# RWKV-7, S5 and ConvFFN layer: inverses in 32x32 blocks, gathered state stores, PSUM banks taken later, and a planner that may hold VectorE

## Chip, cores and metric

The kernel runs on one core of a Trainium2 chip, in one launch. Times are device microseconds of that core; lower is better. Three runs were timed, and one more execution was profiled.

## What is computed

One decoder layer for a prompt of 1024 tokens and 8 sample tokens, all in f32:

```python
proj = rmsnorm(x) @ w_in                 # columns: RWKV | S5 input u | two gates
# RWKV-7, 8 heads x 64, one step per token:
sa = einsum('bhvk,bhk->bhv', S, -kk)
S  = S * w[:, :, None, :] + sa[..., None] * (kk * a)[:, :, None, :] + v[..., None] * k[:, :, None, :]
y  = einsum('bhvk,bhk->bhv', S, r)
# S5, 32 groups x 64 complex states:  s_t = A s_{t-1} + B u_t,  y = Re(C s) + D u
z  = gelu(ys) @ w_glu
x += (sigmoid(g_rw) * rw_out + sigmoid(g_s5) * s5_out) @ w_out
x += (gelu(causal_conv3(a_up)) * b_up) @ w_ffn_out
x += sigmoid(rmsnorm(x) @ w_ple_gate) * (p @ w_ple)
```

It returns the final RMSNorm and the new states, among them the last S5 state of the prompt (`ssm_p`, real and imaginary part) and of the samples (`ssm_s`).

## The kernel before

**Layout.** Features lie on partitions, tokens on the free axis (1032 of them). Every large product is split into high and low halves of its operands, three matmuls for one (`psm<-h1h,whi`, `psm<-h1l,whi`, `psm<-h1h,wlo`): weights are loaded as `wraw`, rounded to `whi` on ScalarE, and the rest `wlo` is made on GpSimd.

**Order of the work.** The code doesn't issue instructions. It records them in a planner, class `Sched` (lines 103 to 420), with a cost, a priority and what they depend on. `run` (line 350) takes the engine that can issue first and, of its instructions that are ready at that moment, the one with the smallest priority number; `issue` (line 374) books its cost. So each engine gets one fixed order, and on the chip it follows it strictly. Every recorded instruction is emitted at line 411, so all have this line in the profile, and tiles tell them apart. All DMAs are issued by SP, also in one order. A DMA is charged a fixed part before and after its bytes. A tile of a pool gets its buffer when the first instruction that names it is issued; `pb` is a pool of three PSUM banks (tag `big`).

**Stages.** First the input projection runs as 34 column tiles (`psm<-h1...`), and beside it the S5 part (`build_s5`, line 970): set-up of the discretisation on VectorE (`s_...`), a scan in levels (`cmac`, lines 1172 to 1182), then for each of four quarters a product (`yp`), a store and read-back through DRAM that changes the layout (`yq<-ys`, `yf<-yq`), a GELU (`zt`), and a store (`zd`). The pool `sp` of S5 must be free before the RWKV part can start (line 720).

**RWKV** (`build_rwkv`, line 1270) goes over 8 units, 4 head pairs x 2 halves of 512 tokens, of 8 chunks of 64 tokens. `stage_a` (line 1328) makes the scaled operands `AR` and `BK`. `stage_g` (line 1399) multiplies them to `Gm`, a 128x128 matrix for each chunk and head, and transposes `BK` and `v` (`tpp`, `vpp`). The upper left 64x64 block of each of the 16 matrices of a unit is then inverted (unit triangular): it is stored to DRAM (`ld`), read back as rows that stand on all partitions that need them (`Lj`), 63 steps on VectorE update `Tm`, a step of several columns as a product into `Tt` and a sum, and the result goes through DRAM again (`xd`) back into `Gm`. `chain` (line 1459) walks the chunks one after another, TensorE and VectorE by turns (`chp`, `pe`, `UV`, `S`); its second product `chp<-pe,Gm` needs the inverse. `post` (line 1509) normalises and gates the unit's result; its gate product is `gps`. The preparation of unit n+1 may run beside the chain of unit n, and both stand ahead of the wide matmuls of the large products, which fill TensorE in between.

**The rest.** S5's GLU (`psm<-zh`), then the output projections and the FFN in two parts of tokens (`parts`, line 751), the first beside the last RWKV units. The RWKV pools must be free before the second part.

Of the kernel before, what the change touches and what calls it, by code (L numbers as in the profile page):

```python
# [58 lines left out]
def _const_cols():  # L59
    c = 0  # L60
    for name, n in (("ident", 128), ("mask", 128), ("bo", 128), ("i64", 64),
                    ("scan", HW), ("tinit", 512), ("ones", 128)):
        CONSTS[name] = (c, n)
        c += n
    return c
# [5 lines left out]
def _consts():  # L71
    out = np.zeros((P, NCON), np.float32)

    def put(name, a):
        c, n = CONSTS[name]
        out[:, c:c + n] = a

    put("ident", np.eye(P))
    i, t = np.arange(64)[:, None], np.arange(64)[None, :]
    put("mask", np.tile(np.concatenate([i < t, i <= t], 1), (2, 1)))  # L80
    put("ones", np.full((P, P), 1.0 / D))
    b = np.kron(np.eye(2), np.ones((64, 64)))
    put("bo", b)
    put("i64", np.tile(np.eye(64), (2, 1)))
    s = np.ones((P, HW))
    s[:, ::CH] = 0
    put("scan", s)

    ti = np.zeros((P, 8, 64))
    for p in range(P):  # L90
        for c in range(8):
            ti[p, c, 8 * c + p // 16] = 1
    put("tinit", ti.reshape(P, 512))
    return out
# [7 lines left out]
class Sched:  # L102
# [10 lines left out]
    SWITCH = 90  # L113
    SETS = {"Exp": (0, 6), "Tanh": (0, 11), "Ln": (5, 6), "Gelu_apprx_tanh": (11,), "Sin": (9,)}
# [235 lines left out]
    def run(self, until):  # L350
        pend, free = self.pend, self.free
        while not until():
# [17 lines left out]
            r, o = min(((c[0], c[1]) for c in cand if c[0] <= t + 1e-6),  # L370
                       key=lambda c: (c[1].prio, c[1].seq))
            self.issue(t, o)

    def issue(self, t, o):
# [17 lines left out]
        if e == "SP":  # L392
            st = max(self.dma_free, t + 700)
            self.dma_free = st + o.tail
            end = self.dma_free + 1000
        else:
            end = t + o.lat
# [572 lines left out]
def build_s5(g, sp, pb, cp, I, O, Ud, Zd, pcs, dscr, dap, dma):  # L970
# [236 lines left out]
    dma(O["ssm_s"][0], er)  # L1207
    dma(O["ssm_s"][1], ei)
# [57 lines left out]
    dma(O["ssm_p"][0], Xr[:, :, 127])  # L1266
    dma(O["ssm_p"][1], Xi[:, :, 127])


def build_rwkv(g, rp, pb, pch, py, I, O, Pd, Wd, Ad, Yd, sg, ssh, omu, pc, pcs, dscr, dap, dma,  # L1270
# [23 lines left out]
    def big(name):  # L1294
        return pb.tile([P, HW], F32, name=name, tag="big")
# [103 lines left out]
    def stage_g(p, hf, a):  # L1399
# [4 lines left out]
        fl = lambda z: z.rearrange("p a b -> p (a b)")  # L1404
        for c4 in range(0, NC, 4):
            gp = [big(f"gp{h}").rearrange("p (c t) -> p c t", t=P) for h in range(2)]
            for j in range(4):
                for h in range(2):
                    hs = slice(64 * h, 64 * h + 64)
                    T.matmul(gp[h][:, j], fl(BK[hs, c4 + j]), fl(AR[hs, c4 + j]),  # L1410
                             start=True, stop=True)
# [3 lines left out]
            for j in range(4):  # L1415
                T.transpose(tp[:, j], fl(BK[:, c4 + j]), ident)
            S.activation(BT[:, c4:c4 + 4], tp, AF.Copy)
            vp = big("vpp").rearrange("p (c t) -> p c t", t=P)
            for c in range(c4, c4 + 4):
                if c == 0:  # L1420
                    T.matmul(vp[64:128, 0], v[:, 0:CH], ident, start=True, stop=True)
                else:
                    T.transpose(vp[:, c - c4], v[:, (c - 1) * CH:(c + 1) * CH], ident)
            S.activation(UV[64:128, c4:c4 + 4], vp[64:128], AF.Copy)

        ld = dscr_ring("ld")
        dma(dap(ld, 0, [[64, 64], [4096, 2 * NC], [1, 64]]),
            Gm[0:64, :, :, 0:64].rearrange("p a b t -> p (a b) t"))
        Tm = rp.tile([P, 8, 64], F32, name="Tm", tag="Tm", bufs=2)
        tmp = rp.tile([P, 8, 64], F32, name="Tt", tag="Tt", bufs=2)  # L1430
        dma(Tm, I["con"][:, nc_:nc_ + 512].rearrange("p (a b) -> p a b", b=64))
        JB = 4
        for j0 in range(0, 63, JB):
            L = rp.tile([P, JB, 64], F32, name="Lj", tag="Lj", bufs=4)
            dma(L, dap(ld, j0 * 64, [[0, 8], [4096, 16], [1, JB * 64]]))
            for j in range(j0, min(j0 + JB, 63)):
                n, w = j // 8 + 1, 63 - j
                if n < 3:
                    for c in range(n):
                        V.scalar_tensor_tensor(Tm[:, c, j + 1:], L[:, j - j0, j + 1:],  # L1440
                                               Tm[:, c, j:j + 1], Tm[:, c, j + 1:],
                                               op0=MUL, op1=ADD)
                    continue
                V.tensor_tensor(tmp[:, :n, :w], L[:, None, j - j0, j + 1:].to_broadcast([P, n, w]),
                                Tm[:, :n, j:j + 1].to_broadcast([P, n, w]), op=MUL)
                V.tensor_tensor(Tm[:, :n, j + 1:], Tm[:, :n, j + 1:], tmp[:, :n, :w], op=ADD)
        xd = dscr_ring("xd")
        dma(dap(xd, 0, [[64, P], [8192, 8], [1, 64]]), Tm)
        dma(Gm[0:64, :, :, 0:64].rearrange("p a b t -> p (a b) t"),
            dap(xd, 0, [[1024, 64], [64, 2 * NC], [1, 64]]))  # L1450
# [4 lines left out]
    def dscr_ring(name):  # L1455
        ring[name] = ring.get(name, -1) + 1
        return dscr(f"{name}{ring[name]}", [16, 64, 64])
# [51 lines left out]
    def post(p, c0, w, parts, bv):  # L1509
# [15 lines left out]
        G.tensor_tensor(y, y, q, op=MUL)  # L1525
# [3 lines left out]
        T.matmul(gp[:, :w], g2[:, p * P:(p + 1) * P], sg[:, c0:c0 + w], start=True, stop=True)  # L1529
# [3 lines left out]
    def sample(p, a):  # L1533
# [6 lines left out]
        t1 = rp.tile(sh, F32, name="st1", tag="Tt", bufs=2)  # L1540
# [169 lines left out]
```

## Time and profile before

| what | before |
|---|---|
| median of 3 runs | 1969.66 us |
| lowest and highest | 1963.52, 1975.32 us |
| the profiled execution | 1970.79 us |
| its span, first to last instruction | 1969.0 us |
| mean granted TensorE clock | 0.963 |
| data moved | 236.69 MB, 181247 packets |

The profiled execution lies 1.13 us above the median. Busy times of engines overlap, so they don't add up to the span. A granted clock of 1.00 is 2.4 GHz, 0.50 is 1.2 GHz; a number in between is the mean over a stretch. In the rows below PE is TensorE, PEld its weight load, DVE is VectorE, ACT ScalarE, POOL GpSimd, and SPq the queue of SP that issues the DMAs. An f32 matmul stands in the trace as two instructions.

### The profile page before, as it was taken

The page shows a single profiled execution, that of the slowest core. Times are in us where ns is not written, and L with a number is a line of the kernel's source. Part 1 is how long each engine was busy: PE and PEld are TensorE (multiplying, and loading weights), DVE is VectorE, ACT ScalarE, POOL GpSimd, SP SyncE. Part 2 cuts the span into 40 slices and gives each one's busy share as a digit, 9 for nine tenths or more (in the row PEclk, how much of TensorE's full clock was granted, in tenths as well). Part 3 has the DMA queues.
Part 4 walks back from the last instruction along what each step waited for, and adds up shares of the span by engine and source line. Part 5 has one row for each costly group of instructions (what it writes and reads, how often), then busy time and mean ns, then how long its engine had stood idle before and what let it go on. Part 6 is the DMA issues. An engine that isn't in the chain of part 4 may idle for free.

```text
span 1969.0 us, 31981 instructions
## 1 busy us (share of the span) xinstructions
PE 1841.3 (94%) x11392; PEld 1621.4 (82%) x11392; DVE 1305.3 (66%) x2803; ACT 839.6 (43%) x1453; POOL 833.0 (42%) x1127
## 2 busy tenths in 40 slices
PE   6999769989989999999998999999989999999987
PEld 5988758968888798777676777787889999999987
DVE  8999225867777698986898965546464444435465
ACT  5222334215523542456562455435445333233364
POOL 4453124203322241373653445656554444444454
PEclk9998879969999999999999999999999999999988
DMA  5554973433342554532423223633342333333222
GB/s 183 154 173 134 132 237 122 128 91 99 114 142 81 182 170 147 184 121 72 130 90 115 80 79 104 221 97 96 92 151 76 97 92 92 95 89 98 88 77 84
DMA packets 181247, 236.69 MB, mean 120 GB/s; under 512 B 56400, under 2 KB 104784, under 8 KB 180944
## 3 DMA queue, kind: packets, MB, share of 16 engines
q1 hardware_dynamic: 181088, 234.65, 39.7%
q8 instruction: 90, 1.47, 0.3%
q14 instruction: 69, 0.57, 0.1%
HBM read 189.75 MB, written 45.02 MB: 119 GB/s over the span
## 4 chain that ended last, share of the span: by engine, by line
PE 63%; DVE 13%; DMA 13%; ACT 4%; issue 4%; POOL 2%; SPq 2%; DVEq 0%; ACTq 0%; POOLq 0%
PE psm L411 53%; PE chp L411 4%; DVE Tm L411 3%; DMA yf<-yq 2%; DVE Tt L411 2%; PE Yps L411 2%; PE gp L411 2%; SPq L411 2%; POOL wlo L411 1%; DMA Lj<-ld 1%; DMA Gm<-xd 1%; DMA wraw<-in_w_ffn_in 1%; DMA xd<-Tm 1%; DVE x L411 1%; ACT L411 1%
## 5 line engine op out<-in xcount | busy, mean ns | idle before, releaser
L411 POOL TENSOR_TENSOR wlo<-wraw,whi 128x512 fp32r<-128x512 f32 (+2 forms) x468 | 594.9, 1274 | 684.4 <-ACT whi L411 645.4
L411 PE MATMUL psm<-act,whi 128*128 128x260 f32 (+1 forms) x2880 | 666.5, 324 | 4.9 <-ACT whi L411 1.5
L411 PEld LDWEIGHTS psm<-act,whi 128*128 128x128 f32 x2880 | 478.9, 190 | 50.4 <-ACT whi L411 4.4
L411 ACT ACTIVATE whi<-wraw 128x512 fp32r<-128x512 f32 (+2 forms) x468 | 279.3, 599 | 560.8 <-PE psm L411 313.6
L411 PE MATMUL psm<-act,wlo 128*128 128x260 f32 (+1 forms) x1440 | 465.5, 324 | 1.7 <-POOL wlo L411 1.1
L411 PE MATMUL psm<-mid,whi 128*128 128x260 f32 (+1 forms) x1344 | 311.2, 324 | 12.0 <-DVE gr L411 4.8
L411 PE MATMUL psm<-h1h,whi 128*128 128x344 f32 x816 | 273.2, 337 | 27.4 <-ACT whi L411 14.9
L411 PEld LDWEIGHTS psm<-act,wlo 128*128 128x128 f32 x1440 | 273.5, 190 | 23.0 <-POOL wlo L411 2.5
L411 PE MATMUL psm<-h1l,whi 128*128 128x344 f32 x816 | 276.1, 338 | 1.9 <-DVE h1l L411 1.8
L411 PE MATMUL psm<-h1h,wlo 128*128 128x344 f32 x816 | 273.7, 336 | 0.4 <-POOL wlo L411 0.4
L411 PEld LDWEIGHTS psm<-mid,whi 128*128 128x128 f32 x1344 | 223.5, 190 | 36.9 <-ACT whi L411 10.5
L411 PE MATMUL psm<-mid,wlo 128*128 128x260 f32 (+1 forms) x672 | 215.8, 323 | 0.4 <-POOL wlo L411 0.4
L411 PEld LDWEIGHTS psm<-h1h,whi 128*128 128x128 f32 x816 | 161.0, 198 | 31.9 <-ACT whi L411 15.2
L411 PEld LDWEIGHTS psm<-h1l,whi 128*128 128x128 f32 x816 | 161.2, 198 | 6.2 <-DVE h1l L411 2.9
L411 PEld LDWEIGHTS psm<-h1h,wlo 128*128 128x128 f32 x816 | 161.1, 197 | 3.9 <-issue 0.9
L411 DVE TENSOR_TENSOR Tm<-Tm,Tt 128x140 f32<-128x140 f32 (+37 forms) x376 | 144.8, 385 | 7.4 <-DVE Tt L411 0.2
L411 DVE TENSOR_TENSOR x<-psm,x 128x260 f32<-128x260 f32 (+1 forms) x160 | 84.2, 531 | 93.8 <-PE psm L411 93.5
L411 DVE TENSOR_TENSOR Tt<-Lj,Tm 128x140 f32<-128x140 f32 (+37 forms) x376 | 138.1, 367 | 7.6 <-DVE ta L411 0.3
L411 PEld LDWEIGHTS psm<-mid,wlo 128*128 128x128 f32 x672 | 127.3, 190 | 12.0 <-POOL wlo L411 2.2
L411 DVE TENSOR_TENSOR ta<-psm,rs 128x260 f32<-128x260 f32 (+1 forms) x66 | 33.9, 515 | 106.8 <-PE psm L411 95.9
L411 ACT ACT_TABLE_LOAD x78 | 100.1, 1283 | 2.1 <-PEq L1701 0.7
L411 DVE SCALAR_TENSOR_TENSOR cv<-ta,par,cv 128x512 f32<-128x512 f32 x88 | 80.1, 911 | 29.9 <-ACT cv L411 29.5
(332 smaller groups left out, 2577.2 us busy)
## 6 DMA issues: line engine op xcount, KB each, us to landing
wraw<-in_w_ffn_in SPq DMA_DIRECT2D x176, 256.0 KB
wraw<-in_w_in SPq DMA_DIRECT2D x68, 256.0 KB
Lj<-ld SPq DMA_DIRECT2D x128, 128.0 KB
wraw<-in_w_ffn_out SPq DMA_DIRECT2D x64, 192.0 KB
gd<-gt SPq DMA_DIRECT2D x16, 516.0 KB
wraw<-in_w_out SPq DMA_DIRECT2D x32, 256.0 KB
wraw<-in_w_ple_gate SPq DMA_DIRECT2D x32, 256.0 KB
wraw<-in_w_ffn_out SPq DMA_DIRECT2D x32, 256.0 KB
```

The source lines that it names most:

```text
L411: o.fn(*o.args, **o.kw)
```

## The change

Five parts, in one diff.

- **State stores.** The sample state is copied on ScalarE into the free tile `x0`, the prompt's last column on VectorE into a new tile `xe`, and these are stored right after the sample step; before, both were stored from inside the large state tile, the prompt's behind the four quarters.
- **Inverses.** Both 32x32 diagonal blocks of each 64x64 block are inverted, 31 steps, with coefficients that come in four transfers a unit. The off-diagonal block then takes a VectorE transpose, 16 matmuls of 32x32 (`mgp<-av,Gm`), a copy, 16 more (`mgp<-Gm,av`) and a copy into `Gm`.
- **PSUM banks.** The matmuls and transposes of `stage_g` that start a bank wait for a one-element memset of the tile that they are copied into, so that no bank is taken while that tile still belongs to an older unit. The gate matmul of `post` waits for a late product in the same way.
- **Planner, VectorE.** `HOLD`: of the instructions that get ready within 130 ns, VectorE takes the most urgent and stands until then.
- **Planner, DMA.** The fixed parts charged to a transfer grow by 200 and 300 ns.

```diff
-                    ("scan", HW), ("tinit", 512), ("ones", 128)):
+                    ("scan", HW), ("tinit", 256), ("ones", 128)):
...
+    HOLD = {"DVE": 130}
...
-            r, o = min(((c[0], c[1]) for c in cand if c[0] <= t + 1e-6),
+            r, o = min(((c[0], c[1]) for c in cand if c[0] <= t + self.HOLD.get(e, 0) + 1e-6),
                        key=lambda c: (c[1].prio, c[1].seq))
-            self.issue(t, o)
+            self.issue(max(t, r), o)
...
         if e == "SP":
-            st = max(self.dma_free, t + 700)
+            st = max(self.dma_free, t + 900)
             self.dma_free = st + o.tail
-            end = self.dma_free + 1000
+            end = self.dma_free + 1300
...
     cmac(er, ei, ab8(apr), ab8(api), x0[:, 0], x0[:, 1], mv8, True)
-    dma(O["ssm_s"][0], er)
-    dma(O["ssm_s"][1], ei)
+
+    for i, e in enumerate((er, ei)):
+        S.activation(x0[:, i], e, AF.Copy)
+        dma(O["ssm_s"][i], x0[:, i])
+    xe = tl("xe", [2, 16], tag="ab")
+    for i, X in enumerate((Xr, Xi)):
+        V.tensor_copy(xe[:, i], X[:, :, 127])
+        dma(O["ssm_p"][i], xe[:, i])
...
-    dma(O["ssm_p"][0], Xr[:, :, 127])
-    dma(O["ssm_p"][1], Xi[:, :, 127])
...
+        free = [G.memset(z, 0.0) for z in (Gm[:, 0, 0, 0:1], BT[:, 0, 0:1], UV[64:128, 0, 0:1])]
+        mm = lambda i, *a: g.rec("PE", "matmul", T.ns.matmul, a, dict(start=True, stop=True),
+                                 (free[i],))
+        tr = lambda i, *a: g.rec("PE", "transpose", T.ns.transpose, a, {}, (free[i],))
...
-                    T.matmul(gp[h][:, j], fl(BK[hs, c4 + j]), fl(AR[hs, c4 + j]),
-                             start=True, stop=True)
+                    mm(0, gp[h][:, j], fl(BK[hs, c4 + j]), fl(AR[hs, c4 + j]))
...
-                T.transpose(tp[:, j], fl(BK[:, c4 + j]), ident)
+                tr(1, tp[:, j], fl(BK[:, c4 + j]), ident)
...
+        gs = Gm.rearrange("p a b t -> p (a b) t")
+        dg = [gs[32 * k:32 * k + 32, :, 32 * k:32 * k + 32] for k in range(2)]
         ld = dscr_ring("ld")
-        dma(dap(ld, 0, [[64, 64], [4096, 2 * NC], [1, 64]]),
-            Gm[0:64, :, :, 0:64].rearrange("p a b t -> p (a b) t"))
-        Tm = rp.tile([P, 8, 64], F32, name="Tm", tag="Tm", bufs=2)
...
-        JB = 4
-        for j0 in range(0, 63, JB):
-            L = rp.tile([P, JB, 64], F32, name="Lj", tag="Lj", bufs=4)
-            dma(L, dap(ld, j0 * 64, [[0, 8], [4096, 16], [1, JB * 64]]))
...
+        for k in range(2):
+            dma(dap(ld, 16384 * k, [[32, 32], [1024, 2 * NC], [1, 32]]), dg[k])
+        Tm = rp.tile([P, 8, 32], F32, name="Tm", tag="Tm", bufs=2)
...
+        L = rp.tile([P, 31, 32], F32, name="Lj", tag="Lj", bufs=1)
+        for r in range(4):
+            dma(L[32 * r:32 * r + 32], dap(ld, 0, [[1024, 32], [1, 31 * 32]]))
+        for j in range(31):
+            n, w = j // 4 + 1, 31 - j
+            if n == 1:
+                V.scalar_tensor_tensor(Tm[:, 0, j + 1:], L[:, j, j + 1:], Tm[:, 0, j:j + 1],
+                                       Tm[:, 0, j + 1:], op0=MUL, op1=ADD)
+                continue
+            V.tensor_tensor(tmp[:, :n, :w], L[:, None, j, j + 1:].to_broadcast([P, n, w]),
+                            Tm[:, :n, j:j + 1].to_broadcast([P, n, w]), op=MUL)
+            V.tensor_tensor(Tm[:, :n, j + 1:], Tm[:, :n, j + 1:], tmp[:, :n, :w], op=ADD)
         xd = dscr_ring("xd")
...
+        dma(dap(xd, 0, [[32, P], [4096, 8], [1, 32]]), Tm)
+        for k in range(2):
+            dma(dg[k], dap(xd, 512 * k, [[1024, 32], [32, 2 * NC], [1, 32]]))
+
+        av = rp.tile([64, 2 * NC, 32], F32, name="av", tag="av", bufs=1)
+        V.transpose(av[0:32], dg[0])
+        mp = big("mgp").rearrange("p (a t) -> p a t", t=32)
+        for j in range(2 * NC):
+            T.matmul(mp[32:64, j], gs[0:32, j, 32:64], av[0:32, j], start=True, stop=True)
+        S.activation(av[32:64], mp[32:64], AF.Copy)
+        mp = big("mgp").rearrange("p (a t) -> p a t", t=32)
+        for j in range(2 * NC):
+            T.matmul(mp[0:32, j], av[32:64, j], gs[32:64, j, 32:64], start=True, stop=True)
+        S.activation(gs[0:32, :, 32:64], mp[0:32], AF.Copy)
         return dict(Gm=Gm, BT=BT, UV=UV)
...
-        G.tensor_tensor(y, y, q, op=MUL)
+        late = G.tensor_tensor(y, y, q, op=MUL)
...
-        T.matmul(gp[:, :w], g2[:, p * P:(p + 1) * P], sg[:, c0:c0 + w], start=True, stop=True)
+        g.rec("PE", "matmul", T.ns.matmul,
+              (gp[:, :w], g2[:, p * P:(p + 1) * P], sg[:, c0:c0 + w]),
+              dict(start=True, stop=True), (late,))
```

How the order changes at three places. A row is an engine's instruction: its line, operation, output and inputs, and the shape of the output, with the number of equal ones behind. Line 411 of before is line 413 of the changed kernel.

SP's queue at the end of S5, before. `out_ssm_p` are the prompt's state stores; `zd`, `yq` and `yf` are the store and the trip of one quarter.

```order
L411 DMA ur<-ud_141 128x1152
L411 DMA cdl<-cdd_607 128x1152
L411 DMA out_ssm_p<-Xr 2048x1x1
L411 DMA out_ssm_p<-Xi 2048x1x1
L411 DMA zd_128<-zt 128x1032
L411 DMA yq_693<-ys 128x1088
L411 DMA yf<-yq_681 128x8x136
L411 DMA wraw<-in_w_in 128x512
```

The state stores of the changed kernel stand earlier in the same queue, ahead of the quarters' loads:

```order
L413 DMA wraw<-in_w_in 128x512
L413 DMA out_ssm_p<-xe 128x16
L413 DMA out_ssm_s<-x_660 128x128 x2
L413 DMA out_ssm_p<-xe 128x16
L413 DMA toep<-kd_594 16x8x128 x7
```

The stores of 2048 pieces are gone, and nothing of the state stands between the quarters' trips any more.

TensorE where the first unit's inverse is first used, before:

```order
L411 MATMUL psm<-h1h,wlo 128x344
L411 MATMUL psm<-h1h,whi 128x344
L411 MATMUL chp<-pe,Gm 64x64 x2
L411 MATMUL psm<-h1l,whi 128x344
...
L411 MATMUL chp<-UV,BT 128x128
L411 MATMUL Yps<-Gm,UV 64x64 x2
```

and the same place now; `gp` are the products of the second unit's `Gm`:

```order
L413 MATMUL gp_2922<-AR,BK 128x128 x4
...
L413 MATMUL mgp<-av,Gm 32x32 x16
L413 MATMUL tpp<-con,BK 128x128 x4
L413 MATMUL psm<-h1h,wlo 128x344
...
L413 MATMUL mgp<-Gm,av 32x32 x16
L413 MATMUL gp_2925<-AR,BK 128x128
L413 MATMUL gp_2926<-AR,BK 128x128
...
L413 MATMUL chp<-pe,Gm 64x64 x2
```

Two groups of small matmuls now stand ahead of the chain's product, with four transposes and nine wide matmuls between the groups and five `gp` products behind them.

VectorE at the start, before; `s_...` is the S5 set-up, `h1h` and `h1l` are TensorE's first operands:

```order
L411 TENSOR_SCALAR h1h<-xin,par 128x1032
L411 SCALAR_TENSOR_TENSOR s_sh<-s_sh,s_mag 128x32
L411 TENSOR_TENSOR s_u_164<-s_ai,ab 128x32
L411 SCALAR_TENSOR_TENSOR h1l<-xin,par,h1h 128x1032
L411 TENSOR_TENSOR s_ar_158<-s_em,s_sh 128x32
```

and now:

```order
L413 TENSOR_SCALAR h1h<-xin,par 128x1032
L413 TENSOR_TENSOR s_sh<-s_sh 128x32
L413 SCALAR_TENSOR_TENSOR s_sh<-s_sh,s_mag 128x32
L413 TENSOR_TENSOR s_ar_158<-s_em,s_sh 128x32
L413 TENSOR_TENSOR s_ai<-s_mag,s_sn 128x32
L413 TENSOR_TENSOR s_u_163<-s_ar_158,ab 128x32
L413 TENSOR_TENSOR s_u_164<-s_ai,ab 128x32
```

The set-up runs in one piece ahead of all `h1l`, instead of by turns with them.

## Rows read from the trace of the kernel before

**Rows 1.** The page: span, and busy time, share and instructions of each engine.

```profile
span 1969.0 us, 31981 instructions
...
PE 1841.3 (94%) x11392; PEld 1621.4 (82%) x11392; DVE 1305.3 (66%) x2803; ACT 839.6 (43%) x1453; POOL 833.0 (42%) x1127
```

**Rows 2.** Stretches: stretch and length, busy (instructions) of each engine, granted clock, DMA share, GB/s.

```profile
200.00:300.00 100.00, 69.90 (x399) 65.99 (x399) 23.88 (x48) 36.25 (x51) 16.30 (x44) 0.85 0.88 180
```

**Rows 3.** Stretches of the RWKV units, columns as above.

```profile
340.00:440.00 100.00, 88.98 (x494) 80.42 (x492) 72.25 (x214) 21.10 (x35) 20.86 (x27) 0.81 0.39 118
440.00:640.00 200.00, 192.47 (x1248) 168.56 (x1247) 154.39 (x451) 83.54 (x134) 59.04 (x84) 0.98 0.35 107
640.00:800.00 160.00, 152.19 (x981) 135.25 (x981) 128.98 (x320) 65.54 (x123) 46.72 (x93) 0.99 0.50 162
800.00:1250.00 450.00, 430.58 (x2075) 321.66 (x2074) 360.32 (x706) 246.38 (x425) 230.72 (x318) 1.00 0.38 119
```

**Rows 4.** TensorE in time: start, length, instruction [idle before it, what ended it].

```profile
221.55 1.70 PE L411 MATMUL yp<-ur,toep 128*128 128x136 f32 x6 [3.30 <-issue]
...
229.09 0.79 PE L411 MATMUL yp<-xs,cdl 128*128 128x136 f32 x2 [4.48 <-DMA cdl<-cdd]
...
258.92 0.65 PE L411 MATMUL psm<-h1h,whi 128*128 128x344 f32 x1 [14.87 <-ACT whi L411]
...
285.88 3.63 PE L411 MATMUL gps<-sg,g 128*128 128x512 f32 x4 [4.29 <-DMA g<-in_g]
...
412.10 0.69 PE L411 MATMUL chp<-pe,Gm 64*64 64x64 f32 x4 [8.95 <-DMA Gm<-xd]
```

**Rows 5.** TensorE's waits over the span: total us, times, longest us.

```profile
PE chp L411 <- DMA Gm<-xd: 24.7, 8, 9.0
```

**Rows 6.** The queue of SP in time, columns as in rows 4.

```profile
216.82 5.59 SPq L411 DMA_DIRECT2D out_ssm_p<-Xi  x1
222.52 6.71 SPq L411 DMA_DIRECT2D zd<-zt  x1
```

**Rows 7.** The chain of waits that ended last: start, length, what (xN instructions).

```profile
78.87 1.85 PE kp L411 x16
...
229.79 25.07 DMA yf<-yq
...
258.84 6.91 DMA yf<-yq
...
324.96 3.13 DMA ld<-Gm
...
329.54 3.46 DMA Lj<-ld
...
404.49 3.87 DMA xd<-Tm
...
408.38 3.68 DMA Gm<-xd
```

**Rows 8.** VectorE's work on the tile Tm over the span: stretch, busy (instructions), clock, DMA.

```profile
0.00:1969.00 1969.00, 336.51 (x944) 0.96 0.40 120
```

**Rows 9.** TensorE in time in the fourth unit's chain, columns as in rows 4.

```profile
640.64 0.44 PE L411 MATMUL chp<-pe,Gm 64*64 64x64 f32 x4 [1.55 <-DMA Gm<-xd]
641.01 0.42 PE L411 MATMUL psm<-h1h,whi 128*128 128x344 f32 x1
641.27 0.32 PE L411 MATMUL psm<-h1l,whi 128*128 128x344 f32 x1
641.43 0.32 PE L411 MATMUL psm<-h1h,wlo 128*128 128x344 f32 x1
...
642.06 0.34 PE L411 MATMUL Yps<-Gm,UV 128*64 128x64 f32 x4
...
642.33 0.43 PE L411 MATMUL psm<-h1l,whi 128*128 128x344 f32 x1
```

**Rows 10.** VectorE in time at the start, columns as in rows 4.

```profile
17.06 2.46 DVE L411 TENSOR_TENSOR s_u<-s_ai,ab 128x32 f32<-128x32 f32 x1
```

More of the change, by code (lines that the diff above doesn't have):

```diff
@@ L87, in _consts @@
     put("scan", s)
-    ti = np.zeros((P, 8, 64))
+    ti = np.zeros((P, 8, 32))
     for p in range(P):
         for c in range(8):
-            ti[p, c, 8 * c + p // 16] = 1
-    put("tinit", ti.reshape(P, 512))
+            ti[p, c, 4 * c + p // 32] = 1
+    put("tinit", ti.reshape(P, 256))
     return out
@@ L1420, in stage_g @@
                 if c == 0:
-                    T.matmul(vp[64:128, 0], v[:, 0:CH], ident, start=True, stop=True)
+                    mm(2, vp[64:128, 0], v[:, 0:CH], ident)
                 else:
-                    T.transpose(vp[:, c - c4], v[:, (c - 1) * CH:(c + 1) * CH], ident)
+                    tr(2, vp[:, c - c4], v[:, (c - 1) * CH:(c + 1) * CH], ident)
             S.activation(UV[64:128, c4:c4 + 4], vp[64:128], AF.Copy)
+        gs = Gm.rearrange("p a b t -> p (a b) t")
+        dg = [gs[32 * k:32 * k + 32, :, 32 * k:32 * k + 32] for k in range(2)]
@@ L1426, in stage_g @@
         ld = dscr_ring("ld")
-        dma(dap(ld, 0, [[64, 64], [4096, 2 * NC], [1, 64]]),
-            Gm[0:64, :, :, 0:64].rearrange("p a b t -> p (a b) t"))
-        Tm = rp.tile([P, 8, 64], F32, name="Tm", tag="Tm", bufs=2)
-        tmp = rp.tile([P, 8, 64], F32, name="Tt", tag="Tt", bufs=2)
-        dma(Tm, I["con"][:, nc_:nc_ + 512].rearrange("p (a b) -> p a b", b=64))
-        JB = 4
-        for j0 in range(0, 63, JB):
-            L = rp.tile([P, JB, 64], F32, name="Lj", tag="Lj", bufs=4)
-            dma(L, dap(ld, j0 * 64, [[0, 8], [4096, 16], [1, JB * 64]]))
[L1436 to L1446, printed above, removed]
@@ L1447, in stage_g @@
-        xd = dscr_ring("xd")
-        dma(dap(xd, 0, [[64, P], [8192, 8], [1, 64]]), Tm)
-        dma(Gm[0:64, :, :, 0:64].rearrange("p a b t -> p (a b) t"),
-            dap(xd, 0, [[1024, 64], [64, 2 * NC], [1, 64]]))
+        for k in range(2):
+            dma(dap(ld, 16384 * k, [[32, 32], [1024, 2 * NC], [1, 32]]), dg[k])
+        Tm = rp.tile([P, 8, 32], F32, name="Tm", tag="Tm", bufs=2)
+        tmp = rp.tile([P, 8, 32], F32, name="Tt", tag="Tq", bufs=2)
+        dma(Tm, I["con"][:, nc_:nc_ + 256].rearrange("p (a b) -> p a b", b=32))
@@ L1456, in dscr_ring @@
         ring[name] = ring.get(name, -1) + 1
-        return dscr(f"{name}{ring[name]}", [16, 64, 64])
+        return dscr(f"{name}{ring[name]}", [32, 32, 32])
     def chain(p, hf, a, b):
@@ L1539, in sample @@
         dma(Sx, I["wkv0"][p])
-        t1 = rp.tile(sh, F32, name="st1", tag="Tt", bufs=2)
+        t1 = rp.tile(sh, F32, name="st1", tag="st1", bufs=1)
         fl = lambda z: z.rearrange("p a b -> p (a b)")
```

## The prediction

> **What bounds the kernel now.** I read the busy times first: over the span of 1969.0 us TensorE is busy for 1841.3 us, VectorE for 66% and ScalarE for 43% [rows 1]. TensorE is idle for 127.7 us in all, so the kernel is TensorE's instruction stream plus its holes, and a saved microsecond on another engine counts only where a hole closes. Next come the stretches [rows 2, 3], whose columns show where holes and low clock lie, then TensorE's own waits with what ended them [rows 4, 5], and last the queue of SP and the chain of waits, for what stood behind a wait [rows 6, 7].
>
> Two places hold most of what can be had. In 200 to 300 us TensorE is busy for 69.9 of 100 us at a mean granted clock of 0.85 [rows 2], a mix of 1.2 and 2.4 GHz in which the slow parts follow holes. In 340 to 1250 us the four stretches add up to 45.8 us without work, and the clock is 0.81 in the first [rows 3]; of this, eight waits of the first triangular product on its inverse, read back from DRAM, take 24.7 us [rows 5].
>
> **The state stores.** The two stores of the prompt's S5 state write 2048 single elements each. The second held SP for 5.59 us and the load or store behind it for 6.71 us [rows 6]. The read-back of yq issued next took 25.07 us to land, where a later one took 6.91 us [rows 7]. ScalarE's weight conversions stand in its queue behind the GELU that waits for that read-back: so TensorE waited 3.30, 4.48 and 14.87 us [rows 4]. The change gathers each state into rows of 16 or 128 contiguous elements first, and puts these stores ahead of three of the four groups of toep loads. The next wait there, 4.29 us, is the gate matmul of `post`, issued long before its data are used, for the load of g2 [rows 4]; the change ties that matmul to a late product. Together 26.9 us. The low clock took 0.15 of 69.9 us of work, 10 us more. I let 6 us stay, one read-back of the ordinary length that shows through: 37 - 6 = **31 us off**.
>
> **The inverses.** Before, a unit's inverse takes 63 column steps on 64x64 blocks; now 31 steps on 32x32 blocks, with the off-diagonal block made by two groups of 16 small matmuls. VectorE's share falls from 944 instructions in 336.5 us [rows 8], 0.356 us each, to 464 by the new order. At that mean they are 165 us, so some 171 us of VectorE's time go. None of it counts by itself. What counts is when TensorE meets the result: the first unit's inverse ran from the store at 324.96 us to its landing at 412.06 us [rows 7], 87 us. Now its four DMA hops at 3.13, 3.46, 3.87 and 3.68 us [rows 7], 14.1 us, and 58 steps at 0.356 us, 20.6 us, make 35 us and what VectorE puts between. In the new order TensorE has some 240 wide matmuls and two dozen others between that unit's last transpose of BK and its first small group; a 344-column matmul starts every 0.16 us [rows 9], so some 40 us: covered, barely.
>
> The planner, though, places the small group close to where it thinks the block is back, so lateness of a hop is a hole again. Before, the lateness was 24.7 / 8 = 3.1 us a unit. The change charges each transfer 0.5 us more, 2.0 us over four hops, so 1.1 us a unit stay, 9 us. The low clock cost 0.19 x 89.0 = 16.9 us in 340 to 440 us, where the longest wait is, 8.95 us [rows 4], and 0.02 x 192.5 + 0.01 x 152.2 = 5.4 us after it [rows 3]. I let 5 us of it stay, as short waits cost that, and 3 us for the new step TensorE to ScalarE to TensorE between the two groups, which a handful of matmuls covers. Before 24.7 + 22.3 = 47 us, after 17: **30 us off**.
>
> **The small matmuls**, 256 in all, are new work on the engine that bounds. No row shows one of 32 columns. From below: 8 matmuls of 128 columns took 1.85 us [rows 7], 0.23 us each, and a quarter of the columns would be 0.058 us, 15 us in all. From above: a pair of 64x64 ones starts 0.37 us before the next instruction [rows 9], 0.185 us each with the change of array shape in it, 47 us in all. The 128x64 pair without that change takes 0.27 us [rows 9], 0.135 us each; this is the nearest row, with twice the columns. I take 0.10 us, between it and the quarter: 25.6 us. Going to the small shape and back costs 0.37 - 0.27 = 0.10 us each way, 16 groups: 3 us. **29 us on.** The Trainium skill, TensorEngine Tiling (Array Packing), section Instruction Overhead, speaks against this: it gives each matmul some 60 cycles of overhead, so that a free dimension of 1 takes as long as 60. By it 32 columns would cost what 64 do, and the sum would be 9 us higher; no row decides it.
>
> **The rest.** At the start the small S5 set-up instructions stood between the wide ones that make TensorE's first operands; one of 32 columns took 2.46 us beside GpSimd's work [rows 10]. The planner now lets VectorE stand for up to 130 ns so that the set-up finishes first, while the inputs are still on their way. From nothing to two such instructions, 0 to 5 us: 3 us off. In 800 to 1250 us 19.4 us are without work [rows 3]; with VectorE freer a quarter may close: 5 us off. Standing itself costs VectorE, which has a third of the span free [rows 1]; TensorE is fed by it, so from 3 us off to 5 on, and I take 0. The extra ScalarE copies, three one-element memsets a unit and the gathering copies cost nothing beside ScalarE's 43%; if that cover goes, a copy of half a microsecond stands before a chain, 8 us. SP's rows fall from 662 to 551, since a unit loads its coefficients in 4 transfers, not 16; packets of the hops shrink from 256 to 128 bytes at the same number, for which I take the old durations.
>
> **Sum**, on the profiled execution's 1970.8 us (1.1 us above the median shown): -31 - 30 + 29 - 3 - 5 = -40, so **1931 us**.
>
> **Rivals.**
> *Flat price:* the small matmuls cost what 64 columns cost, 256 x 0.135 + 3 = 38 us: 1940 us. For: each needs its own weight load, as those do. Against: the 128-column row is dearer in proportion to its columns. The page above states this one.
> *The S5 tail stays serial:* the yq round trips stand behind one another, and ScalarE's weight conversions behind each; three at 6.91 us [rows 7] come back as holes, 20 of the 31 us: 1951 us. Against: before 25 us were frozen, these trips ran under matmuls.
> *The stores were not the cause:* the late read-back comes from the 16 toep loads ahead of it, and the 31 us do not come: 1962 us. Against it: SP itself was held behind the store before that read-back was issued [rows 6].
> *Full cover:* no inverse wait is left (17 us more), and another 16 us close: 1898 us.
> *Slower:* TensorE meets each small group too early. The group now stands ahead of the whole chain, and a late block holds all matmuls behind it. With 6 us a unit and 4 us of work at half clock, 80 us instead of 17: 1994 us. It decides from 7 us lost a unit; the first unit shows 8.95 us and 17 of clock, the others 2.2 us on average, and the 35 us against some 40 leave little.
>
> **How the numbers follow.** Forecast 0.48, flat price 0.15, serial tail 0.14, full cover 0.10, slower 0.09, not the cause 0.04. The range goes from full cover to just past "not the cause", 1900 to 1963 us; the mishap at 1994 lies outside, with a part of the spread of the others. A difference under 0.5% (10 us) can't be told from none. Faster than 1961: the forecast, flat price and full cover nearly whole, and three quarters of the serial tail, 0.81; within 10 us, the rest of these and most of "not the cause", 0.10; slower 0.09.
>
> **What would show it.** Right: no stretch between 200 and 300 us in which DVE, ACT and POOL all stand, TensorE's busy time there above 90 us, and no load in it that takes over 10 us to land; waits of the small groups of 1 to 3 us, together under 15, and no granted clock under 0.9 over 340 to 440 us; VectorE's steps near 165 us; the small groups at 1.6 us per 16. Wrong: a wait of more than 5 us before a small group, followed by half clock; groups at 2.5 us or more; a frozen stretch after the S5 scan.

## The result, and the profile after

The changed kernel takes **1907.58 us** (median of 4 runs, 1904.99 to 1926.42) against 1972.49 us for the kernel before, run beside it: a ratio of 0.9691, 95% interval 0.9613 to 0.9769. Run once more (after_again) it took 1905.7 us, ratio 0.9691 [0.9660, 0.9721]. The profiled execution took 1906.36 us, 64.4 us less than the one profiled before; 40 were forecast. Here and below, an execution more than 1.5% above the fastest of its kernel is left out of ratios and medians (five of ten in u_hold and in d_mgp, two of four in d_sparse). The page of the profile, then its stretches (columns as in [rows 2]):

```profile
span 1904.6 us, 32427 instructions
...
PE 1829.4 (96%) x11904; PEld 1624.1 (85%) x11904; DVE 1159.5 (61%) x2333; ACT 832.3 (44%) x1461; POOL 847.0 (44%) x1151
```

```profile
0.00:50.00 50.00, 32.16 (x162) 29.46 (x163) 44.93 (x94) 28.33 (x36) 23.80 (x49) 0.90 0.50 180
200.00:300.00 100.00, 88.58 (x550) 86.39 (x549) 39.37 (x75) 46.73 (x70) 31.23 (x62) 0.93 0.70 216
340.00:440.00 100.00, 96.20 (x736) 78.67 (x734) 70.55 (x209) 43.54 (x76) 23.07 (x36) 0.95 0.29 86
440.00:640.00 200.00, 197.52 (x1416) 163.07 (x1415) 138.52 (x405) 97.16 (x172) 59.92 (x97) 0.94 0.27 78
640.00:800.00 160.00, 158.05 (x1143) 135.24 (x1141) 108.89 (x245) 94.67 (x171) 62.17 (x124) 1.00 0.43 132
800.00:1250.00 450.00, 443.69 (x2135) 361.42 (x2134) 251.06 (x374) 189.26 (x328) 232.29 (x299) 1.00 0.39 124
```

TensorE is idle for 75.2 us (1904.6 - 1829.4), 52.5 less than [rows 1] give, and busy for 11.9 us less, although it does 256 matmuls more (512 instructions). Both halves count: an idle microsecond is a wait, and the busy time shrinks or grows with the clock. Against [rows 2, 3], the hole of 200 to 300 us went from 30.1 to 11.4 us, those of 340 to 1250 us from 45.8 to 14.5 us, and 0.81 of the clock in 340 to 440 us became 0.95; but 440 to 640 us, once at 0.98, now stands at 0.94.

The waits of TensorE that have to do with an inverse (columns as in [rows 5]) stood at 24.7 us; now these are all:

```profile
PE chp L413 <- ACT Gm L413: 1.5, 2, 1.0
...
PE mgp L413 <- ACT av L413: 0.7, 1, 0.7
PE vps L413 <- ACT Gm L413: 0.7, 1, 0.7
...
PE mgp L413 <- DVE av L413: 0.5, 2, 0.3
```

The first unit's small groups in time (as in [rows 4]; x32 are 16 matmuls), the second with the wait for ScalarE's copy between them:

```profile
352.58 0.32 PE L413 MATMUL psm<-h1l,whi 128*128 128x344 f32 x1
352.83 1.19 PE L413 MATMUL mgp<-av,Gm 32*32 32x32 f32 x32
353.95 0.66 PE L413 MATMUL tpp<-con,BK 128*128 128x128 f32 x4
...
356.79 1.19 PE L413 MATMUL mgp<-Gm,av 32*32 32x32 f32 x32 [0.75 <-ACT av L413]
357.91 0.93 PE L413 MATMUL gp<-AR,BK 64*128 64x128 f32 x10
```

A group holds TensorE for 1.12 us, 0.07 us a matmul; all 16 groups are busy for 19.04 us. VectorE's steps on `Tm` came down to 128.00 us (x464). SP's queue shows the four state stores at once (x2 is two of them), and what used to be [rows 6] is gone; the read-backs of yq land in 6.80 and 6.22 us where one took 25.07 [rows 7]:

```profile
195.25 0.34 SPq L413 DMA_DIRECT2D out_ssm_p<-xe  x1
195.68 0.86 SPq L413 DMA_DIRECT2D out_ssm_s<-x  x2
196.63 1.18 SPq L413 DMA_DIRECT2D out_ssm_p<-xe  x1
```

And the clock: in three adjoining stretches of the same execution it is half for 24 us, with TensorE busy all through:

```profile
460.00:473.00 13.00, 12.39 (x98) 9.20 (x95) 9.49 (x18) 11.45 (x21) 8.08 (x16) 1.00 0.56 179
473.00:497.00 24.00, 24.00 (x111) 18.05 (x107) 11.37 (x25) 9.35 (x16) 3.88 (x6) 0.52 0.16 41
497.00:510.00 13.00, 12.05 (x81) 9.58 (x80) 9.86 (x24) 4.51 (x9) 4.45 (x11) 0.97 0.17 59
```

### The profile page after: what moved, and what is told of

Its sections match the earlier page's. It is cut to its first block, busy times and chain, and to the rows that moved or that the text cites. A ratio compares the mean times of both kernels' runs of the same rounds, so it can differ in the third digit from the quotient of the medians.

```text
span 1904.6 us, 32427 instructions
## 1 busy us (share of the span) xinstructions
PE 1829.4 (96%) x11904; PEld 1624.1 (85%) x11904; DVE 1159.5 (61%) x2333; ACT 832.3 (44%) x1461; POOL 847.0 (44%) x1151
## 4 chain that ended last, share of the span: by engine, by line
PE 77%; DVE 9%; DMA 6%; ACT 3%; issue 2%; POOL 1%; SPq 1%; DVEq 0%; POOLq 0%; ACTq 0%
PE psm L413 65%; PE chp L413 4%; PE Yps L413 2%; DVE Tm L413 1%; PE gp L413 1%; DVE Tt L413 1%; PE yp L413 1%; DVE x L413 1%; SPq L413 1%; DMA yf<-yq 1%; POOL wlo L413 1%; PE mgp L413 1%; ACT L413 1%; DVE m L413 1%; DVE Xi L413 1%
## 5 line engine op out<-in xcount | busy, mean ns | idle before, releaser
L413 PE MATMUL psm<-act,whi 128*128 128x260 f32 (+1 forms) x2880 | 655.2, 322 | 3.3 <-ACT whi L413 2.3
L413 PE MATMUL psm<-mid,whi 128*128 128x260 f32 (+1 forms) x1344 | 307.0, 321 | 2.0 <-ACT mid L413 2.0
L413 PE MATMUL psm<-h1l,whi 128*128 128x344 f32 x816 | 272.1, 334 | 2.0 <-DVE h1l L413 2.0
L413 DVE SCALAR_TENSOR_TENSOR cv<-ta,par,cv 128x512 f32<-128x512 f32 x88 | 88.8, 1009 | 40.5 <-ACT cv L413 39.0
L413 DVE TENSOR_TENSOR mid<-cv,mid 128x260 fp32r<-128x260 f32 (+1 forms) x84 | 69.5, 832 | 29.1 <-ACT mid L413 28.8
L413 ACT ACTIVATE sw<-S,WC 64x64 f32<-64x64 f32 x120 | 41.3, 344 | 73.1 <-DVE S L413 71.4
```

Of the source, the lines that this page charges most:

```text
L413: o.fn(*o.args, **o.kw)
```

## The experiments

First each part was undone alone in the changed kernel, then what this left open was tested. "Idle" and "busy" are TensorE's in the profiled execution; ratio is to the kernel before, run on the same chip. Chips differ (the kernel before took 1961.1, 1966.5 and 1964.7 us beside the three sets), so ratios are compared, with the medians beside. A profile is of one execution: that of u_dma is the longest of its four (1951.29 us), those of h0_late and half_late are the shortest of theirs.

| kernel | median us | ratio [95%] | idle | busy | clock |
|---|---|---|---|---|---|
| before (profiled) | 1969.66 | 1 | 127.7 | 1841.3 | 0.963 |
| changed | 1907.58 | 0.9691 [0.9613, 0.9769] | 75.2 | 1829.4 | 0.973 |
| after_again | 1905.70 | 0.9691 [0.9660, 0.9721] | 77.2 | 1824.8 | 0.977 |
| u_stores | 1927.21 | 0.9831 [0.9778, 0.9884] | 92.9 | 1833.7 | 0.970 |
| st_place | 1936.68 | 0.9850 [0.9809, 0.9890] | 106.1 | 1823.6 | 0.971 |
| u_inverse | 1912.83 | 0.9767 [0.9724, 0.9811] | 96.7 | 1812.2 | 0.977 |
| o_inverse | 1939.95 | 0.9870 [0.9824, 0.9916] | 90.0 | 1842.4 | 0.971 |
| u_psum | 1914.29 | 0.9785 [0.9734, 0.9836] | 84.7 | 1825.9 | 0.983 |
| half_late | 1932.85 | 0.9838 [0.9796, 0.9881] | 80.4 | 1841.4 | 0.972 |
| u_dma | 1944.27 | 0.9881 [0.9826, 0.9935] | 93.8 | 1855.7 | 0.958 |
| u_hold | 1934.40 | 0.9854 [0.9807, 0.9901] | 67.7 | 1864.9 | 0.956 |
| h0_late | 1935.16 | 0.9857 [0.9807, 0.9907] | 78.6 | 1846.6 | 0.967 |
| d_mgp | 1958.03 | 0.9925 [0.9881, 0.9968] | 76.9 | 1879.3 | 0.956 |
| d_sparse | 1942.94 | 0.9885 [0.9812, 0.9958] | 78.8 | 1885.8 | 0.958 |

**The changed kernel again** (no edit):

> The changed kernel once more, unchanged, on the chip of the runs beside it: 1900 to 1927 us, as in the first comparison, and the spread of its executions with the clock of each, against which the others are read.

It took 1903.76 to 1910.24 us, with clocks of 0.970 to 0.977: the slowest execution has the lowest clock. The order is the same, but the clock falls at other places. Behind 340 us the changed kernel's first profile has 10 us at half clock from 361 us and 24 us from 474 us; this one has 3 us from 361 us and 24 us from 409 us, and none in 440 to 640 us:

```profile
340.00:440.00 100.00, 96.16 (x685) 78.12 (x685) 63.55 (x187) 40.65 (x70) 20.50 (x34) 0.86 0.28 80
440.00:640.00 200.00, 197.93 (x1485) 164.43 (x1483) 144.47 (x423) 101.53 (x178) 63.41 (x100) 1.00 0.29 85
```

The fall at 409 us comes inside the second small group of the second unit (first row here); the first profile ran the same instructions, with the same ones ahead of them, at full clock (second row):

```profile
408.00 1.43 PE L413 MATMUL mgp<-Gm,av 32*32 32x32 f32 x32
```

```profile
411.69 1.19 PE L413 MATMUL mgp<-Gm,av 32*32 32x32 f32 x32
```

So what stands just before a fall doesn't settle whether it comes, and one profile doesn't show where an order draws half clock. The readings of single falls below are to be taken with this.

**The stores as before** (u_stores), and the old form at the new place (st_place):

```diff
-    for i, e in enumerate((er, ei)):
-        S.activation(x0[:, i], e, AF.Copy)
-        dma(O["ssm_s"][i], x0[:, i])
-    xe = tl("xe", [2, 16], tag="ab")
-    for i, X in enumerate((Xr, Xi)):
-        V.tensor_copy(xe[:, i], X[:, :, 127])
-        dma(O["ssm_p"][i], xe[:, i])
+    dma(O["ssm_s"][0], er)
+    dma(O["ssm_s"][1], ei)
...
+    dma(O["ssm_p"][0], Xr[:, :, 127])
+    dma(O["ssm_p"][1], Xi[:, :, 127])
```

In u_stores the last two lines stand behind the four quarters, in st_place right behind the first two.

> The changed kernel with the four S5 state stores as before: strided single elements, the prompt's behind the four quarters. If the stores were the cause of the 31 us (theory): 1938 us, between 1930 and 1948, with TensorE back to some 70 to 75 us of work in the 100 us around the S5 tail and one load there that takes over 20 us to land. Rival, the stores were not the cause and the new order carries the gain: 1904 to 1914 us, and no load over 10 us.

> The changed kernel with the S5 states stored from inside the state tile, element by element, but at the new place in the program, right after the sample step and ahead of three of the four groups of toep loads. Theory (it is the form of the store that blocks, wherever it stands): some 25 us in which loads issued behind it do not land, now earlier, and most of the 20 us that the old stores cost: 1920 to 1932 us. Rival (the place decides: ahead of the toep loads the block falls under TensorE's remaining input projection): 1903 to 1914 us, though the slow stores show in SP's queue.

u_stores is slower by 0.014 of the ratio (28 us; 21.5 by the medians), st_place by 0.016 (31 us). Both lie beside their theory's range, u_stores 3 us under it and st_place 5 us over, and far from the rivals'. SP's queue shows the block: in u_stores (first fence) the read-back behind the last store waits 12.95 us, in st_place (second) the toep loads wait 27.62 us, and TensorE (third) waits for them.

```profile
236.16 0.55 SPq L413 DMA_DIRECT2D out_ssm_p<-Xi  x1
236.80 12.95 SPq L413 DMA_DIRECT2D yq<-ys  x1
```

```profile
199.55 1.01 SPq L413 DMA_DIRECT2D out_ssm_p<-Xr  x1
200.60 1.16 SPq L413 DMA_DIRECT2D out_ssm_p<-Xi  x1
201.86 27.62 SPq L413 DMA_DIRECT2D toep<-kd  x8
```

```profile
234.09 1.70 PE L413 MATMUL yp<-ur,toep 128*128 128x136 f32 x6 [31.39 <-DMA toep<-kd]
```

So it is the form of the store that blocks, at either place; with the old form the new place gains nothing. Gathered stores at the old place were not run, and both kernels undo the sample's stores along with the prompt's. One expected sign failed: in u_stores the longest transfer of the chain of waits there took 16.63 us, not over 20.

**The inverse as before in the changed kernel** (u_inverse), **and the new inverse alone in the kernel before** (o_inverse). The edit is the whole part on inverses of the diff shown above, backwards and forwards; its core:

```diff
-        L = rp.tile([P, 31, 32], F32, name="Lj", tag="Lj", bufs=1)
-        for r in range(4):
-            dma(L[32 * r:32 * r + 32], dap(ld, 0, [[1024, 32], [1, 31 * 32]]))
-        for j in range(31):
...
+        JB = 4
+        for j0 in range(0, 63, JB):
+            L = rp.tile([P, JB, 64], F32, name="Lj", tag="Lj", bufs=4)
+            dma(L, dap(ld, j0 * 64, [[0, 8], [4096, 16], [1, JB * 64]]))
```

> The changed kernel with the inverse as before: 64x64 blocks, 63 steps, coefficients in 16 transfers a unit, no small matmuls. By the prediction's terms the inverses give 30 us and the small matmuls take 29, so this kernel would run as the changed one: 1901 to 1912 us. By what the profile after shows (inverse waits down by some 20 us, clock over 340 to 440 us up, small groups 18 us and not 26): 1920 to 1930 us. Rival, VectorE's freed 190 us are what closes holes all over: 1935 us or more, with VectorE waits spread over the RWKV part.

> The kernel before with the blocked inverse alone: old stores, no HOLD, banks as before, the old charge for transfers. By the prediction's terms the inverse saves 30 and its small matmuls cost 29, so no change: ratio to before 0.995 to 1.005. By what undoing it in the changed kernel cost (7 us by the medians, 15 by the ratios): ratio 0.990 to 0.996, with no wait left on a product that needs an inverse. Rival (without HOLD the small groups land in running chains and the clock falls): ratio 1.005 or more.

Undone, it costs 0.0076 of the ratio (15 us; 7 by the medians), 1 us outside what the prediction's terms gave; alone it gives 0.013, 25 us, more than any of the three expectations. In both the waits on an inverse are short: u_inverse, with the *old* inverse, shows of the 24.7 us only

```profile
PE chp L413 <- DMA Gm<-xd: 1.6, 4, 0.6
```

and o_inverse, with the old charge for transfers and no HOLD, has 6.3 us (`mgp<-av`: 4.6 + 1.7). The prediction had the planner's charge close two thirds of the lateness and gave the shorter inverse no part in it. With the shorter inverse alone 6.3 of the 24.7 us are left, with the rest of the change alone 1.6: either closes most of it, and the second adds little. Whether in u_inverse it is the charge, HOLD or the late banks that close it, no run separates.

**The planner's charge for DMAs as before** (u_dma, the first two pairs of lines), **HOLD at 0** (u_hold, the third), **banks and gate matmul free** (u_psum, the last two; `(free[i],)` is taken out at both its places):

```diff
-            st = max(self.dma_free, t + 900)
+            st = max(self.dma_free, t + 700)
...
-            end = self.dma_free + 1300
+            end = self.dma_free + 1000
...
-    HOLD = {"DVE": 130}
+    HOLD = {"DVE": 0}
...
-                                 (free[i],))
+                                 ())
...
-              dict(start=True, stop=True), (late,))
+              dict(start=True, stop=True), ())
```

> The changed kernel with the planner's charge for a transfer as before, 0.5 us less a hop. By the prediction's term (2.0 us of lateness saved a unit over four hops): waits of the small groups and of the first chain product up by 10 to 16 us in all, 1915 to 1924 us. Rival (lateness was not what the charge decided, since the groups now stand far from their loads): under 5 us of such waits, 1900 to 1912 us unless the new order brings more half clock, which the clock would show.

> The changed kernel with HOLD at 0, so VectorE takes what is ready first. Theory: standing costs VectorE nothing and gives TensorE nothing, 1901 to 1912 us. Rival, the part that was priced at 0 carries the 24 us that the prediction missed: 1925 us or more, with longer waits for VectorE before the chain's products and the first operands.

> The changed kernel with the matmuls that start a bank, and the gate matmul of post, free to go as early as their operands allow. Theory: one wait of some 4 us behind a load returns, and matmuls that wait for a copy into an older unit's tile, 1906 to 1916 us. Rival, late banks are what keeps TensorE fed in 440 to 800 us: 1920 us or more, with waits of stage_g's matmuls of over 2 us each.

u_dma: 38 us slower by either measure, but its inverse waits are 2.8 us, so lateness is not the reason, as its rival had it. It has some 17 us more of other waits and 26 to 31 us more busy time at a clock of 0.958. Its longest stretch at half clock has neither a wait nor a small group in the 20 us before it, only products of the chain and of `gp` among wide ones:

```profile
774.00:804.00 30.00, 30.00 (x132) 23.05 (x132) 9.94 (x29) 10.15 (x25) 2.88 (x8) 0.50 0.13 32
```

u_hold: 32 us by the ratio, 29 by the medians, the time of its rival but not its reason: the whole of it is busy time, and it has the *fewest* idle microseconds of all, 67.7. One of its ten executions took 4802.57 us at a clock of 1.00; no trace of it is there, and it stays unexplained. Three stretches of u_hold, again full of work:

```profile
620.00:634.00 14.00, 14.00 (x123) 10.80 (x122) 5.72 (x23) 5.04 (x11) 1.38 (x2) 1.00 0.37 105
634.00:666.00 32.00, 32.00 (x158) 24.57 (x157) 7.98 (x24) 9.39 (x18) 4.23 (x8) 0.52 0.01 2
666.00:680.00 14.00, 14.00 (x94) 10.14 (x93) 8.43 (x23) 9.02 (x16) 8.05 (x12) 1.00 0.25 94
```

What TensorE did just before the fall: small groups cut into the steps of a running chain, hardly a wide matmul between.

```profile
631.18 0.62 PE L413 MATMUL mgp<-av,Gm 32*32 32x32 f32 x14
631.74 0.49 PE L413 MATMUL chp<-UV,BT 128*128 128x128 f32 x2
632.15 0.34 PE L413 MATMUL Yps<-Gm,UV 128*64 128x64 f32 x4
632.42 0.37 PE L413 MATMUL mgp<-av,Gm 32*32 32x32 f32 x6
632.72 0.43 PE L413 MATMUL psm<-h1l,whi 128*128 128x344 f32 x1
633.08 0.43 PE L413 MATMUL chp<-S,AR 128*64 128x128 f32 x2
633.44 0.44 PE L413 MATMUL chp<-UV,Gm 64*64 64x64 f32 x4
633.81 0.43 PE L413 MATMUL Yps<-AR,S 128*128 128x64 f32 x2
634.05 0.46 PE L413 MATMUL psm<-h1h,wlo 128*128 128x344 f32 x1
634.45 0.42 PE L413 MATMUL mgp<-Gm,av 32*32 32x32 f32 x4
634.79 0.69 PE L413 MATMUL chp<-pe,Gm 64*64 64x64 f32 x4
```

Two chain matmuls of 64x64 (x4) take 0.69 us at half clock and 0.44 before. In u_hold four of the eight units have their groups inside a running chain, and behind all four the clock is half; in the changed kernel no group stands so. But the clock also fell at three of the other four groups of u_hold (at 347, 487 and 778 us). u_psum: 9 us by the medians, 18 by the ratio; its spread-out order shows no half clock from 300 to 900 us, and pays in idle time (84.7), with a hole of 4.59 us at 1393 us, where the second part of the tokens waits for RWKV's end. The wait of the gate matmul for its load, gone in the changed kernel, is back as the theory had it:

```profile
278.31 3.65 PE L413 MATMUL gps<-sg,g 128*128 128x512 f32 x4 [2.79 <-DMA g<-in_g]
```

**HOLD 0, with the groups kept out of the chains** (h0_late): each first group waits for the last product of the chain before it.

```diff
+                end = T.matmul(Y[hs, c], UV[:, c, hs], Gm[:, c, h, 64:128], start=first, stop=True)
...
+        if n + 1 < len(units):
+            with g.prio(base(n + 1, 0)):
+                small(nxt[1], (end,))
```

> HOLD at 0, and one thing more: a unit's first small group waits for the last product of the chain before it, so that no small group stands inside a running chain. Theory (what HOLD 0 lost was the clock: in that profile four of the eight units have their small groups inside a running chain, with 30 to 44 small matmuls about them, and the clock falls to half behind each of these): no fall behind a small group but at most one or two, mean clock 0.97 or more, 1905 to 1922 us. Rival (HOLD 0 costs by VectorE's order itself, the chains being served late): 1930 us or more, with a clock as good as in the changed kernel and longer waits of TensorE for VectorE.

1935 us, 0.9857, about where u_hold was: the rival's time, but not its reason. Idle time is that of the changed kernel (78.6), so HOLD 0 does not make VectorE serve the chains late; the loss is again half clock. But falls remain: behind the small groups at 348 us (a wait of 0.65 us ahead), 396 and 532 us (both close behind a chain's last step, with `gp` products after them). Forbidding the place inside the chain was not enough, and the theory in that form fell.

**Each small matmul twice**, in the changed kernel (d_mgp) and in the order of u_psum (d_sparse):

```diff
-            T.matmul(mp[32:64, j], gs[0:32, j, 32:64], av[0:32, j], start=True, stop=True)
+            for _ in range(2):
+                T.matmul(mp[32:64, j], gs[0:32, j, 32:64], av[0:32, j], start=True, stop=True)
```

> The changed kernel with each of the 256 small matmuls issued twice, with the same result. By the 0.07 us each that the profile shows (1.15 us for 16): 18 us more, 1922 to 1930 us. Rival (they stand in time that would be idle): under 6 us more. Second rival (dense small work brings half clock): 30 us more or beyond, with new falls of the granted clock within some us behind the doubled groups.

> The 256 small matmuls doubled once more, but on the kernel whose banks and gate matmul are free to go early (u_psum, 1914 us, no fall of the clock over 300 to 900 us). [...] Theory (half clock comes from dense small work, not from the number of small matmuls): the 18 us of the matmuls themselves and no more, 1928 to 1938 us, clock 0.975 or more. Rival (any group of 32 or more small matmuls in a row brings the fall): 1950 us or more, clock 0.96 or less, as when the changed kernel's groups were doubled.

d_mgp costs 0.0234 of the ratio, 46 us (52 by the medians), as its second rival had it: the groups take 39.82 us instead of 19, and the rest is half clock. Its ten executions run from 1937.02 us at a clock of 0.967 to 1987.63 us at 0.941. d_sparse was to show that wide work all round protects. It is 20 us slower than u_psum by the ratios and 29 by the medians, between its theory and its rival; its four executions run from 1933.14 us at a clock of 0.974, as the theory had it, to 1976.09 at 0.949. So the times don't decide. In the profiled one, 1966.45 us at 0.958, the clock fell at the first group of four units out of six up to 850 us. One of them:

```profile
351.32 0.32 PE L413 MATMUL psm<-h1h,whi 128*128 128x344 f32 x1
352.75 2.18 PE L413 MATMUL mgp<-av,Gm 32*32 32x32 f32 x64 [1.11 <-DVE av L413]
354.86 0.43 PE L413 MATMUL psm<-h1l,whi 128*128 128x344 f32 x1
355.12 0.32 PE L413 MATMUL psm<-h1h,wlo 128*128 128x344 f32 x1
355.29 0.36 PE L413 MATMUL psm<-h1h,whi 128*128 128x344 f32 x1
355.44 0.49 PE L413 MATMUL psm<-h1l,whi 128*128 128x344 f32 x1
```

Wide matmuls stand before and behind it, yet from 355.4 us a wide one takes 0.49 us, and this lasts to 380 us. The four units with a fall had a wait of 0.92 to 1.75 us just ahead of the group, as here; of the two without, one had none (619.37 us) and one had 1.21 us. So wide work beside a group doesn't always protect, and what these four falls share is a wait and a small group side by side. Neither is needed, though. The longest fall of the same profile, 31 us from 560 us, has no wait and no small group in the 15 us before it. And in u_inverse, which has no small group at all, the clock fell behind a wait of the same length between wide matmuls (first row; the second is the stretch behind it):

```profile
944.49 0.72 PE L413 MATMUL psm<-mid,whi 128*128 128x512 f32 x2 [1.41 <-ACT whi L413]
```

```profile
946.00:949.00 3.00, 2.87 (x7) 1.66 (x6) 1.86 (x6) 1.27 (x2) 1.68 (x4) 0.50 0.40 132
```

That one lasted 3.4 us, where those beside a group lasted 10 to 24 us.

**Half the units with a late gate matmul** (half_late), an attempt at a faster version:

```diff
-              dict(start=True, stop=True), (late,))
+              dict(start=True, stop=True), (late,) if lt else ())
...
-            post(p, hf * HW, HW, y, a["bv"])
+            post(p, hf * HW, HW, y, a["bv"], n >= 4)
```

> The changed kernel with the late gate matmul only in the four units of the second 512 tokens; the first four may take their bank early. This lies between two measured kernels: with all eight late RWKV ends early and small work stands dense (clock falls, no hole before the second part); with none late it is spread out, without falls, and a hole of 4.6 us stands before the second part. Theory: some of both, fewer falls and no hole over 4 us before the second part, 1898 to 1908 us, faster than the changed kernel by 0 to 8 us. Rival (the gain of one is the loss of the other): 1906 to 1914 us.

Both expectations missed: 1932.85 us. Behind a small group at 678 us, with a wait of 1.39 us ahead of it, the clock fell for 24 us, at 811 us for 3 us more, and from 917 us for 20 us with no small group near. No kernel run here beats the changed one.

## Why the prediction was right, and what it mis-sized

The range (1900 to 1963 us) and the sign held; the forecast was 24 us too high. In the profile's two halves: it had 42 us of idle time go and 2 us of busy time come; 52.5 went, and busy time fell by 11.9. That the sum came this near is in part luck. Against its terms, 10 us more of idle time closed, the small matmuls cost 10 us less, and the clock gave back some 18 us less; these nearly cancel. A further 21 us went that no term names (last point).

- **State stores, 31 us.** Right in mechanism, place and nearly in size: undoing them costs 21.5 us by the medians, 28 by the ratio. "Not the cause" and "the tail stays serial" are out: no freeze, read-backs at 6 to 7 us, three waits of `yp` for loads are left, 2.8, 2.7 and 1.9 us. TensorE's busy time there, 88.58 us, is just short of the sign of 90, and 6.2 us of half clock stayed (0.07 x 88.6) where all 10 were to go. The two stores' part is shown; that of the gate matmul is 2.8 us (u_psum), not 4.3.
- **The lateness left to the inverses, 9 + 3 us.** Mis-sized: 3.4 us (the waits above). The step that failed is "The change charges each transfer 0.5 us more, 2.0 us over four hops, so 1.1 us a unit stay, 9 us": it let the charge alone close the lateness. With the shorter inverse and the old charge 2.8 us are left (u_dma), with the old inverse and the new charge 1.6 (u_inverse).
- **Small matmuls, 29 us.** Mis-sized: 19.04 us, 0.07 us each and not 0.10. This lies near the lower bound, a quarter of the 128-column row. The 64-column row, taken as the nearest, was the wrong neighbour. The rule of the Trainium skill, TensorEngine Tiling (Array Packing), section Instruction Overhead, read for f32 as the prediction did (32 columns cost what 64 do), is not what this trace shows: 0.07 against 0.135 us.
- **VectorE at 165 us.** 128.00 us: the steps also became shorter, 0.276 against 0.356 us.
- **Half clock, 5 us left to stay in 340 to 800 us.** Missed in size and, for the greater part, in kind. 4.8 us stay in 340 to 440 us (0.05 x 96.2) and 11.9 us in 440 to 640 us (0.06 x 197.5), 12 us more than allowed. The first stands behind waits of 0.75 and 0.98 us for a step of the inverse and one of 1.39 us for VectorE, much as the term had it. The second has one wait of 0.61 us ahead of it and otherwise products of the chain and `gp`. In after_again the same order loses 13.5 us in the first stretch (0.14 x 96.2) and nothing in the second; "no granted clock under 0.9 over 340 to 440 us" holds for the mean of one profile (0.95) and not for the other (0.86).
- **Start, 3 us, and 800 to 1250 us, 5 us.** The start gave nothing (TensorE's first 50 us: 32.16 busy, before 33.69). The later stretch gave 13 us of idle time (19.4 to 6.3), with VectorE's busy time there down from 360 to 251 us. This goes with the inverse: TensorE is idle there for 20 us with the old inverse in the changed kernel (u_inverse), and for 7.7 us with the new one alone (o_inverse).
- **HOLD at 0.** Its own cost was taken as nothing either way; undoing it costs 29 to 32 us. It changes where the small groups stand, which the prediction did not price; but with the groups kept out of the chains the time was the same (h0_late). The rival "slower" had one ingredient, half clock round the small groups, and put it down to late blocks; in u_hold the small groups' waits are 2.3 us in all.
- **What stays open.** TensorE is busy at half clock for 102.9 us in the trace before and for 83.8 us in the changed kernel's (65.4 in after_again). Taken at full clock, its work would be 1789.8 us before and 1787.5 after (1792.2); less 19 us of small groups, 17 to 21 us too little. Part of it can be read by tile: the same 256 instructions of `gp` take 40.11 us before and 30.40 after, the same 4320 of `psm<-act` 722.72 and 698.45. With the banks free again (u_psum) they are back at 36.15 and 722.13, so much of it goes with the late banks, to which no term gave this. Fewer changes of array shape ([rows 9] price one at 0.10 us) don't explain it: counted in the two traces there are 581 before and 596 after. Why it is so, no run shows.
- **What a part is worth** stays open too. Undone one by one, the five parts cost 105 us by the medians and 130 by the ratios, about twice what they gain together (65 us). All five kernels that alter the planner's order alone (u_hold, h0_late, u_dma, u_psum, half_late) are slower, by 9 to 39 us in the medians, four of them mainly by busy time at a lower clock. Whether HOLD helps as a rule or this one order is a lucky one, no run shows.

## What to carry to other kernels

Two remedies for the same wait don't add up: ask of each what it would do alone, and again with the other in place. When a hole on TensorE is closed with small matmuls, price what they do to the clock as well as their own time, and look where the scheduler puts them; a reordered program is best judged by idle and busy time apart, for the clock shows in the second alone, and by several executions, for one order draws half clock here in one and there in another. Gather a strided state into contiguous rows before it is stored: here the block came from the form of the store, not from its place.

## What the hardware showed that was not expected

- The granted clock falls to half without any hole: at 634 us in u_hold and at 474 us in the changed kernel behind dense small products (the latter with a 0.61 us wait at 471.20 us), and stays there for 31 and 24 us although TensorE is busy throughout. In u_dma at 774 us no wait and no 32x32 matmul stood in the 20 us before, and it stayed for 30 us.
- The same program draws different clocks: d_mgp's ten executions differ by 51 us, from a clock of 0.967 to 0.941; the changed kernel's four beside the first comparison by 21 us. The same order had its longest fall at 474 us in one profile and at 409 us in another.
- A 32x32 by 32-column f32 matmul costs 0.07 us in a run of 16, half of a 64-column one in another array shape ([rows 9], 0.135 us).
- Two stores of 2048 single elements take up to 28.6 us to land (st_place; 27.6 in u_stores) and hold the transfers behind them on SP for 27.62 us (12.95 in u_stores), against 2.4 us of SP's time for all four states when gathered.
